# The first token tile's products of v for four pieces of weights, ahead of the second tile's x

## The chip, the cores and the metric

The kernel runs on one core of a Trainium2 chip. The metric is the device time of one execution in microseconds (us). TensorE (PE in the profile; PEld is its weight load) multiplies, VectorE (DVE), ScalarE (ACT) and GpSimd (POOL) work elementwise, SyncE (SP) issues the loads. Each engine works through its own instructions in the order of the program.

## The reference

One block of a network on `x` of 256 tokens by 1024 features, all in float32: an RMSNorm, a wide projection `w_in`, causal pooling and block attention side by side, gates, an output projection, and an MLP with squared ReLU.

```python
u = rmsnorm(h, norm_mix_pre[l])
z = u @ w_in[l]
p = z[..., :o_q]
q = z[..., o_q:o_k].reshape(B, S, N_HEADS, HEAD_DIM)
k = z[..., o_k:o_v].reshape(B, S, N_HEADS, HEAD_DIM)
v = z[..., o_v:o_g].reshape(B, S, N_HEADS, HEAD_DIM)
...
h = h + rmsnorm(m @ w_out[l], norm_mix_post[l])
u2 = rmsnorm(h, norm_mlp_pre[l])
a = jnp.square(jax.nn.relu(u2 @ w_up[l]))
h = h + rmsnorm(a @ w_down[l], norm_mlp_post[l])
```

What the change touches is the start: `v = u @ w_in[:, v columns]`, a product of 256 x 1024 by 1024 x 512.

## The kernel before, in words

**Three products for one.** Every float32 operand is split in a high part of reduced precision and a low part (operand minus high part). A product is then three matmuls: high by high, and the two mixed ones. `mm3` (L223) issues these three; in the text they are "a triple".

**The v stage.** The tokens lie in two tiles t = 0, 1 of 128 rows, the 1024 features in eight pieces k of 128. The weights of v are eight loads of 128 x 512 (`load_v(k)`, `v_r` in the trace, 256 KB each). x comes in four loads of 256 KB: `load_x(t, n)` takes tile t, half n of the features, so that half 0 serves k = 0 to 3 and half 1 serves k = 4 to 7. For v,

- `turn_x(t, n)` (L348) transposes four 128 x 128 blocks of x on TensorE into one PSUM bank (`x_ps`);
- `u_parts(k, t)` (L336) makes the two parts of u from that bank, scaled by the norm's gain: `uh` on ACT (L307), then `ul` on DVE (L308), which reads uh;
- `split_v(k)` (L351) splits a piece of weights: `v_h` on ACT (L89), then `v_l` (L93), of whose 512 columns DVE makes 352 and POOL 160;
- `v_rows(t, k)` (L341) is the triple that adds piece k into tile t's accumulator `v_ps`. It needs uh and v_h for its first matmul, both shares of v_l for the second and ul for the third (v_h, ul).

The 1/rms factor of a token is applied when v leaves PSUM, so the products don't wait for it. The whole program is written in the order that each engine follows (`manual_schedule`, L40): an instruction that waits holds up all that stand behind it on its engine. Some matmuls on constants (`keep_busy`, L59) fill TensorE until the first x has come.

**Loads.** SP issues all loads of weights and x on one queue. Eight semaphores are used in turn, so an issue waits until the load eight places ahead of it has landed. `load_next` (L145) issues the next block of weights of the list that begins with q, k and p; it takes one of three raw buffers and waits until the block in that buffer is split.

**Behind v.** The four pieces of q's weights are split (`q_h` on ACT, `q_l` on DVE and POOL) right behind the last `u_parts`; TensorE multiplies q (32 triples of 256 columns), then k, scores, p and so on. DVE makes the token norms between q_l and the splits of k's weights (`k_l`, L406), which are followed by what it takes out of q's and k's accumulators.

Of the kernel before, what the change touches and what calls it, by code (L numbers as in the profile page):

```python
# [20 lines left out]
KD = D // P  # L21
# [12 lines left out]
def hybrid_block(ctx: ExitStack, tc: tile.TileContext, x, norm_mix_pre, w_in, b_gate, pool_w, pool_scale,  # L34
# [110 lines left out]
    def load_next():  # L145
        if done[0] < len(order):
            order[done[0]].load_all()
            done[0] += 1
# [15 lines left out]
    def load_x(t, n):  # L164
        c = slice(n * 512, (n + 1) * 512)
        nc.sync.dma_start(x_sb[:, t, c], x[0, t * P:(t + 1) * P, c])


    class Columns:
# [12 lines left out]
        def turn(self):  # L182
            ps = bank(self.name + "_ps")
            nc.tensor.transpose(ps[:, 0:self.n], self.row, ident[0:self.n, 0:self.n])
            nc.vector.tensor_copy(self.col, ps[:, 0:self.n])
# [8 lines left out]
    def load_v(k):  # L194
        bv[k // 4].load(k % 4)

    load_x(0, 0)
    g_mix.load()
    load_v(0)
    load_v(1)  # L200
    load_x(1, 0)
    load_v(2)
    load_x(0, 1)
    load_v(3)
    load_x(1, 1)
    for k in range(4, KD):
        load_v(k)
    load_next()
    others.load()
# [13 lines left out]
    def mm3(ps, whl, rhl, start, stop, last=0):  # L223

        (wh, wl), (rh, rl) = whl, rhl
        second, third = ((wh, rl), (wl, rh)) if last == 0 else ((wl, rh), (wh, rl))
        nc.tensor.matmul(ps, wh, rh, start=start, stop=False, skip_group_check=True)  # L227
        nc.tensor.matmul(ps, *second, start=False, stop=False, skip_group_check=True)  # L228
        nc.tensor.matmul(ps, *third, start=False, stop=stop, skip_group_check=True)  # L229
# [12 lines left out]
    def tokens(hl, k, t):  # L242
        c = slice(t * P, (t + 1) * P)
        return hl[0][:, k, c], hl[1][:, k, c]
# [5 lines left out]
    def narrow(blocks, k, c=slice(0, 512)):  # L250
        b = blocks[k // 4]
        return b.hi[:, k % 4, c], b.lo[:, k % 4, c]
# [50 lines left out]
    def scaled_parts(hl, k, t, ps, gain):  # L303
        c = slice(t * P, (t + 1) * P)
        v = ps[:, (k % 4) * P:(k % 4 + 1) * P]
        hi, lo = hl[0][:, k, c], hl[1][:, k, c]
        nc.scalar.activation(hi, v, AF.Copy, scale=gain)  # L307
        nc.vector.scalar_tensor_tensor(lo, v, gain, hi.bitcast(F32), op0=ALU.mult, op1=ALU.subtract)  # L308
# [27 lines left out]
    def u_parts(k, t):  # L336
        scaled_parts(u, k, t, xT[t, k // 4], g_mix[k])
# [3 lines left out]
    def v_rows(t, k, last=0):  # L341
        mm3(vps[t], tokens(u, k, t), narrow(bv, k), k == 0, k == KD - 1, last)
# [5 lines left out]
    def turn_x(t, n):  # L348
        xT[t, n] = turn(x_sb[:, t, :], n, f"x_ps{t}{n}")

    def split_v(k):  # L351
        bv[k // 4].split_piece(k % 4, True)
# [5 lines left out]
    u_parts(0, 0)  # L358
    bv[0].share_lo(0)
    v_rows(0, 0, last=1)  # L360
    u_parts(1, 0)
    turn_x(1, 0)
    split_v(1)
    v_rows(0, 1)
    u_parts(0, 1)
    v_rows(1, 0)
    turn_x(0, 1)
    u_parts(1, 1)
    v_rows(1, 1)
    for k in range(2, KD):  # L370
        if k == 3:
            turn_x(1, 1)
        split_v(k)
        for t in range(NT):
            u_parts(k, t)
            v_rows(t, k)
        if k == 3:
            load_next()
    for b in bq:
        b.allot()  # L380
    bq[0].split_piece(0, True)
# [521 lines left out]
```

## Time and profile before

| | |
|---|---|
| median of 3 runs | 350.66 us (350.08 to 565.49) |
| the profiled execution, its own time | 350.98 us |
| its span, from first to last instruction | 349.2 us |
| mean granted TensorE clock | 0.992 |
| v's first matmul to its last (starts) | 5.57 to 19.68 us |
| q's first matmul | 20.18 us |

The profile counts time from the first instruction. In a line of the timeline the first number is an instruction's start, the second its duration; several alike in a row are put together (xN). What stands in brackets is the idle time of the engine just before, and what ended it. Matmuls are pipelined: a 128 x 512 one is shown with 0.39 us, and the next starts 0.23 us after it.

### The profile page before, as it was taken

The page shows a single profiled execution, that of the slowest core. Times are in us where ns is not written, and L with a number is a line of the kernel's source. Part 1 is how long each engine was busy: PE and PEld are TensorE (multiplying, and loading weights), DVE is VectorE, ACT ScalarE, POOL GpSimd, SP SyncE. Part 2 cuts the span into 40 slices and gives each one's busy share as a digit, 9 for nine tenths or more (in the row PEclk, how much of TensorE's full clock was granted, in tenths as well). Part 3 has the DMA queues.
Part 4 walks back from the last instruction along what each step waited for, and adds up shares of the span by engine and source line. Part 5 has one row for each costly group of instructions (what it writes and reads, how often), then busy time and mean ns, then how long its engine had stood idle before and what let it go on. Part 6 is the DMA issues. An engine that isn't in the chain of part 4 may idle for free.

```text
span 349.2 us, 5700 instructions
## 1 busy us (share of the span) xinstructions
PE 337.0 (96%) x2313; PEld 309.5 (89%) x2313; DVE 216.0 (62%) x284; ACT 182.0 (52%) x257; POOL 98.7 (28%) x80
## 2 busy tenths in 40 slices
PE   7999999999999999899999999999999999999991
PEld 6799999999999999678899898998989989899880
DVE  2889687995474476656677846537465374653545
ACT  3885657665557442447775635445254452544231
POOL 3599966143113088718530000000000000000000
PEclk9999999999999999999999999999999999999996
DMA  6996861552636636563467490935709358090003
GB/s 203 382 288 232 195 229 38 218 164 95 225 122 240 240 122 243 153 209 121 139 223 234 160 331 12 340 131 211 272 9 340 134 199 283 8 346 11 0 0 120
DMA packets 27506, 63.04 MB, mean 181 GB/s; under 512 B 1332, under 2 KB 3160, under 8 KB 27480
## 3 DMA queue, kind: packets, MB, share of 16 engines
q1 hardware_dynamic: 26904, 62.15, 51.3%
q0 software_dynamic: 576, 0.52, 1.1%
q8 instruction: 18, 0.29, 0.3%
q14 instruction: 8, 0.07, 0.1%
HBM read 61.10 MB, written 1.05 MB: 178 GB/s over the span
## 4 chain that ended last, share of the span: by engine, by line
PE 55%; DVE 1%; ACT 0%; DVEq 0%; issue 0%; ACTq 0%
PE up_ps L227 8%; PE up_ps L228 8%; PE up_ps L229 8%; PE d_ps L240 8%; PE d_ps L236 8%; PE d_ps L237 8%; PE wo_ps L240 1%; PE wo_ps L237 1%; PE wo_ps L236 1%; PE d_ps L229 1%; PE d_ps L228 1%; PE d_ps L227 1%; PE h_ps L300 0%; DVE o_out L848 0%; DVE ml L318 0%; PE wo_ps L228 0%
## 5 line engine op out<-in xcount | busy, mean ns | idle before, releaser
L227 PE MATMUL up_ps<-u2h,up_h 128*128 128x256 f32 x224 | 62.2, 278 | 0.0
L228 PE MATMUL up_ps<-u2l,up_h 128*128 128x256 f32 x224 | 62.0, 277 | 0.0
L229 PE MATMUL up_ps<-u2h,up_l 128*128 128x256 f32 x224 | 61.9, 277 | 0.0
L845 POOL TENSOR_TENSOR o_out<-o_out,g_mlp_post 128x256 f32<-128x256 f32 x2 | 1.5, 733 | 164.1 <-DVE rr L289 159.9
L236 PE MATMUL d_ps<-dn_h,ah 128*128 128x512 f32 x120 | 46.9, 391 | 0.0
L93 DVE TENSOR_TENSOR dn_l<-dn_r,dn_h 128x2048 fp32r<-128x2048 f32 x16 | 36.5, 2292 | 16.7 <-ACT dn_h L89 16.7
L237 PE MATMUL d_ps<-dn_l,ah 128*128 128x512 f32 x120 | 46.8, 390 | 0.0
L228 PEld LDWEIGHTS up_ps<-u2l,up_h 128*128 128x128 f32 x224 | 42.1, 188 | 0.3
L227 PEld LDWEIGHTS up_ps<-u2h,up_h 128*128 128x128 f32 x224 | 42.0, 188 | 0.3
L229 PEld LDWEIGHTS up_ps<-u2h,up_l 128*128 128x128 f32 x224 | 42.1, 188 | 0.0
L89 ACT ACTIVATE dn_h<-dn_r 128x2048 fp32r<-128x2048 f32 x16 | 30.5, 1916 | 21.5 <-issue 13.2
L240 PE MATMUL d_ps<-dn_h,al 128*128 128x512 f32 x120 | 37.4, 393 | 0.0
L227 PE MATMUL g_ps<-uh,g_h 128*128 128x256 f32 x128 | 36.6, 286 | 0.6 <-DVE pt L422 0.6
L229 PE MATMUL g_ps<-uh,g_l 128*128 128x256 f32 x128 | 36.2, 283 | 0.0
L228 PE MATMUL g_ps<-ul,g_h 128*128 128x256 f32 x128 | 36.2, 283 | 0.0
L93 DVE TENSOR_TENSOR up_l<-up_r,up_h 128x2048 fp32r<-128x2048 f32 (+1 forms) x14 | 30.2, 2194 | 8.1 <-ACT up_h L89 8.1
L89 ACT ACTIVATE up_h<-up_r 128x2048 fp32r<-128x2048 f32 x16 | 29.9, 1903 | 1.6 <-PE wo_ps L240 1.6
L758 ACT ACTIVATE relu<-up_ps 128x512 f32<-128x512 f32 x16 | 9.5, 594 | 39.8 <-PE up_ps L229 39.8
L760 DVE TENSOR_TENSOR a<-up_ps,relu 128x512 f32<-128x512 f32 x16 | 11.0, 690 | 29.2 <-ACT relu L758 29.1
L240 PEld LDWEIGHTS d_ps<-dn_h,al 128*128 128x128 f32 x120 | 22.5, 188 | 4.9
L237 PEld LDWEIGHTS d_ps<-dn_l,ah 128*128 128x128 f32 x120 | 22.5, 188 | 4.9
L236 PEld LDWEIGHTS d_ps<-dn_h,ah 128*128 128x128 f32 x120 | 22.5, 188 | 4.5
(226 smaller groups left out, 856.3 us busy)
## 6 DMA issues: line engine op xcount, KB each, us to landing
up_r<-in_w_up_dram SPq DMA_DIRECT2D x16, 1024.0 KB, 5.5
dn_r<-in_w_down_dram SPq DMA_DIRECT2D x16, 1024.0 KB, 5.1
g_r<-in_w_in_dram SPq DMA_DIRECT2D x8, 1024.0 KB, 5.8
o_r<-in_w_out_dram SPq DMA_DIRECT2D x4, 1024.0 KB, 4.9
v_r<-in_w_in_dram SPq DMA_DIRECT2D x8, 256.0 KB, 5.9
q_r<-in_w_in_dram SPq DMA_DIRECT2D x4, 512.0 KB, 6.4
k_r<-in_w_in_dram SPq DMA_DIRECT2D x2, 1024.0 KB, 6.1
p_r<-in_w_in_dram SPq DMA_DIRECT2D x2, 1024.0 KB
```

What stands on the lines that cost most here:

```text
L89: nc.scalar.activation(self.hi[:, s, :], self.raw[:, s, :], AF.Copy)
L93: eng.tensor_tensor(self.lo[:, s, c], self.raw[:, s, c], self.hi[:, s, c].bitcast(F32), ALU.subtract)
L227: nc.tensor.matmul(ps, wh, rh, start=start, stop=False, skip_group_check=True)
L228: nc.tensor.matmul(ps, *second, start=False, stop=False, skip_group_check=True)
L229: nc.tensor.matmul(ps, *third, start=False, stop=stop, skip_group_check=True)
L236: nc.tensor.matmul(ps, xh, wh[:, c], start=start, stop=False, skip_group_check=True)
L237: nc.tensor.matmul(ps, xh, wl[:, c], start=False, stop=False, skip_group_check=True)
L240: nc.tensor.matmul(ps, xl, wh[:, c], start=False, stop=stop, skip_group_check=True)
L758: nc.scalar.activation(r, ps, AF.Relu)
L760: nc.vector.tensor_tensor(a, ps, r, ALU.mult)
L845: nc.gpsimd.tensor_tensor(o[:, 768:D], o[:, 768:D], g_mlp_post[:, 768:D], ALU.mult)
```

## The change

The loads of v's pieces 2 and 3 are issued ahead of the second tile's x (and of the first tile's second half). The products of tile 0 with pieces 1 to 3 then run ahead of everything of tile 1. Tile 1 follows with its pieces 0 to 3 in a row; its transpose now stands directly ahead of its first product, and the transpose of its second half directly ahead of its product with piece 4. From piece 5 on the order is that of before. No instruction is added or removed; behind v the order is the same.

```diff
     load_x(0, 0)
     g_mix.load()
-    load_v(0)
-    load_v(1)
+    for k in range(4):
+        load_v(k)
     load_x(1, 0)
-    load_v(2)
     load_x(0, 1)
-    load_v(3)
+    load_v(4)
     load_x(1, 1)
-    for k in range(4, KD):
+    for k in range(5, KD):
         load_v(k)
     load_next()
...
     v_rows(0, 0, last=1)
-    u_parts(1, 0)
+
+    for k in range(1, 4):
+        u_parts(k, 0)
+        split_v(k)
+        v_rows(0, k)
+    load_next()
     turn_x(1, 0)
-    split_v(1)
-    v_rows(0, 1)
     u_parts(0, 1)
     v_rows(1, 0)
-    turn_x(0, 1)
     u_parts(1, 1)
     v_rows(1, 1)
-    for k in range(2, KD):
-        if k == 3:
-            turn_x(1, 1)
-        split_v(k)
+    turn_x(0, 1)
+    u_parts(2, 1)
+    v_rows(1, 2)
+    split_v(4)
+    u_parts(3, 1)
+    v_rows(1, 3)
+    u_parts(4, 0)
+    v_rows(0, 4)
+    turn_x(1, 1)
+    split_v(5)
+    u_parts(4, 1)
+    v_rows(1, 4)
+    for k in range(5, KD):
+        if k > 5:
+            split_v(k)
         for t in range(NT):
             u_parts(k, t)
             v_rows(t, k)
-        if k == 3:
-            load_next()
```

On SP, at the start of the program, before and then after. `x_sb` is x, `v_r` a piece of v's weights:

```order
L166 DMA x_sb<-in_x_dram 128x512
L179 DMA g_mix_row<-in_norm_mix_pre_dram 8x128
L80 DMA v_r<-in_w_in_dram 128x512 x2
L166 DMA x_sb<-in_x_dram 128x512
L80 DMA v_r<-in_w_in_dram 128x512
L166 DMA x_sb<-in_x_dram 128x512
L80 DMA v_r<-in_w_in_dram 128x512
L166 DMA x_sb<-in_x_dram 128x512
L80 DMA v_r<-in_w_in_dram 128x512 x4
```

```order
L166 DMA x_sb<-in_x_dram 128x512
L179 DMA g_mix_row<-in_norm_mix_pre_dram 8x128
L80 DMA v_r<-in_w_in_dram 128x512 x4
L166 DMA x_sb<-in_x_dram 128x512 x2
L80 DMA v_r<-in_w_in_dram 128x512
L166 DMA x_sb<-in_x_dram 128x512
L80 DMA v_r<-in_w_in_dram 128x512 x3
```

Of the twelve loads of 256 KB, tile 1's first half of x moves from the fourth place to the sixth, pieces 2 and 3 from the fifth and seventh to the fourth and fifth.

On TensorE, behind the first triple of v, before: the transposes of x (`x_ps10` is tile 1, half 0; `x_ps01` tile 0, half 1) and the triples of tile 0 (`v_ps0`) and tile 1 (`v_ps1`):

```order
L300 MATMUL x_ps10_192<-ident_110,x_sb_115 128x128 x4
L227 MATMUL v_ps0_159<-v_0_h_161,uh_155 128x512
L228 MATMUL v_ps0_159<-v_0_l_162,uh_155 128x512
L229 MATMUL v_ps0_159<-v_0_h_161,ul_156 128x512
L227 MATMUL v_ps1_160<-v_0_h_161,uh_155 128x512
L228 MATMUL v_ps1_160<-v_0_l_162,uh_155 128x512
L229 MATMUL v_ps1_160<-v_0_h_161,ul_156 128x512
L300 MATMUL x_ps01_208<-ident_110,x_sb_115 128x128 x4
```

And in the changed kernel, the last of three triples of tile 0 in a row and what follows it:

```order
L226 MATMUL v_ps0_159<-v_0_h_161,uh_155 128x512
L227 MATMUL v_ps0_159<-v_0_l_162,uh_155 128x512
L228 MATMUL v_ps0_159<-v_0_h_161,ul_156 128x512
L299 MATMUL x_ps10_217<-ident_110,x_sb_115 128x128 x4
L226 MATMUL v_ps1_160<-v_0_h_161,uh_155 128x512
L227 MATMUL v_ps1_160<-v_0_l_162,uh_155 128x512
L228 MATMUL v_ps1_160<-v_0_h_161,ul_156 128x512
```

Three triples now stand ahead of tile 1's transpose, and no triple of tile 0 between that transpose and the first triple that reads its result. The same holds further on for the second half (`x_ps11`):

```order
L228 MATMUL v_ps0_159<-v_4_h_163,ul_156 128x512
L299 MATMUL x_ps11_255<-ident_110,x_sb_115 128x128 x4
L226 MATMUL v_ps1_160<-v_4_h_163,uh_155 128x512
L227 MATMUL v_ps1_160<-v_4_l_164,uh_155 128x512
L228 MATMUL v_ps1_160<-v_4_h_163,ul_156 128x512
```

Before, a triple of tile 0 stood between these transposes and the triple of tile 1 that needs them.

## Rows read from the trace of the kernel before

**Rows 1.** The page, part 1: busy us, share of the span, instructions of each engine.

```profile
PE 337.0 (96%) x2313; PEld 309.5 (89%) x2313; DVE 216.0 (62%) x284; ACT 182.0 (52%) x257; POOL 98.7 (28%) x80
```

**Rows 2.** Waits of TensorE, whole span: us in total, times, longest us.

```profile
PE wo_ps L236 <- ACT mh L317: 1.0, 1, 1.0
...
PE wo_ps L237 <- POOL o_l L93: 0.7, 1, 0.7
PE g_ps L227 <- DVE pt L422: 0.6, 1, 0.6
```

**Rows 3.** Timeline of TensorE in the v stage and behind it.

```profile
6.56 0.47 PE L229 MATMUL v_ps<-v_l,uh 128*128 128x512 f32 x1 [0.26 <-DVE v_l L93]
7.93 0.66 PE L300 MATMUL x_ps<-ident,x_sb 128*128 128x128 f32 x4 [0.90 <-DMA x_sb<-in_x_dram]
8.35 0.48 PE L227 MATMUL v_ps<-v_h,uh 128*128 128x512 f32 x1
...
12.65 0.60 PE L300 MATMUL x_ps<-ident,x_sb 128*128 128x128 f32 x4
13.00 0.47 PE L227 MATMUL v_ps<-v_h,uh 128*128 128x512 f32 x1
...
20.00 0.24 PE L184 MATMUL others_ps<-ident,others_row 28*128 28x28 f32 x1
20.18 0.39 PE L227 MATMUL q_ps<-uh,q_h 128*128 128x256 f32 x1
...
31.91 0.36 PE L227 MATMUL k_ps<-uh,k_h 128*128 128x256 f32 x1
```

**Rows 4.** Timeline of ScalarE in the v stage.

```profile
5.98 0.62 ACT L89 ACTIVATE v_h<-v_r 128x512 fp32r<-128x512 f32 x1
8.63 0.37 ACT L307 ACTIVATE uh<-x_ps,g_mix_col 128x128 fp32r<-128x128 f32 x1 [2.03 <-PE x_ps L300]
9.41 0.37 ACT L307 ACTIVATE uh<-x_ps,g_mix_col 128x128 fp32r<-128x128 f32 x1 [0.42 <-DVE ul L308]
...
12.09 0.63 ACT L89 ACTIVATE v_h<-v_r 128x512 fp32r<-128x512 f32 x1 [0.21 <-DMA v_r<-in_w_in_dram]
...
13.29 0.37 ACT L307 ACTIVATE uh<-x_ps,g_mix_col 128x128 fp32r<-128x128 f32 x1 [0.30 <-PE x_ps L300]
...
16.61 3.99 ACT L89 ACTIVATE q_h<-q_r 128x1024 fp32r<-128x1024 f32 x4
```

**Rows 5.** Timeline of GpSimd, then of VectorE, same stretch and behind it.

```profile
6.67 0.86 POOL L93 TENSOR_TENSOR v_l<-v_r,v_h 128x160 fp32r<-128x160 f32 x1 [0.65 <-ACT v_h L89]
...
17.79 6.04 POOL L93 TENSOR_TENSOR q_l<-q_r,q_h 128x320 fp32r<-128x320 f32 x4 [0.59 <-ACT q_h L89]
...
5.60 0.82 DVE L93 TENSOR_TENSOR v_l<-v_r,v_h 128x352 fp32r<-128x352 f32 x1
...
26.03 0.16 DVE L286 RECIPROCAL r<-sq 128x1 f32<-128x1 f32 x1 [0.88 <-ACT sq L281]
...
28.10 5.09 DVE L93 TENSOR_TENSOR k_l<-k_r,k_h 128x2048 fp32r<-128x2048 f32 x2
...
60.16 1.27 DVE L422 TENSOR_TENSOR pt<-p_ps,rrow 128x512 f32<-128x512 f32 x2
```

**Rows 6.** Issues on SP's queue, fifth and sixth load; then each one's us to landing.

```profile
2.94 0.43 SPq L80 DMA_DIRECT2D v_r<-in_w_in_dram  x1
3.41 0.43 SPq L166 DMA_DIRECT2D x_sb<-in_x_dram  x1
...
v_r<-in_w_in_dram SPq DMA_DIRECT2D x1, 256.0 KB, 5.6
x_sb<-in_x_dram SPq DMA_DIRECT2D x1, 256.0 KB, 6.6
```

**Rows 7.** Windows: stretch, its length, busy us (instructions) by engine, granted clock, DMA share, GB/s.

```profile
7.00:8.00 1.00, 0.10 (x2) 0.07 (x2) 0.16 (x1) 0.00 (x0) 0.53 (x1) 1.00 0.86 279
...
343.00:344.00 1.00, 0.00 (x0) 0.00 (x0) 0.90 (x5) 0.56 (x2) 0.08 (x1) 0.77 0.00 0
```

## The prediction

> **What bounds the kernel now.** I read four things in this order. The page's first part [rows 1]: TensorE is busy for 337.0 of 349.2 us, so nothing but TensorE's own idle time and the length of its work can move the end. TensorE's waits [rows 2]: behind the start only small ones are left, 1.0, 0.7 and 0.6 us being the longest. So a change in the v stage is worth what it does to the moment at which TensorE gets through that stage, unless one of these later waits takes it back. The timeline of TensorE [rows 3] then shows the stage itself: the first triple ends at 6.56 + 0.23 = 6.79, the transpose of tile 1's x waits for its load until 7.93, and from there TensorE is dense: ten triples between 13.00 and 20.00, 0.70 us each (0.69 without the slower restart behind a transpose), and a transpose costs 0.35 to 0.45 (12.65 to 13.00; 7.93 to 8.35). The hole of 1.14 us from 6.79 to 7.93 is all that the new order can fill. Last, the timelines of ACT, POOL and DVE [rows 4, 5] show what a triple needs before it can run.
>
> **Loads.** The change moves loads between places of one queue, all of 256 KB, so I let a place keep its landing time. The fourth load, now x of tile 1, lands at 7.9 [rows 3]; the fifth at 2.94 + 5.6 = 8.5 and the sixth at 3.41 + 6.6 = 10.0 [rows 6]; the ninth, weight piece 4, ends a wait of ACT at 12.1 [rows 4]; the two between them at 10.7 and 11.4 by equal steps. After the change piece 2 lands at 7.9, piece 3 at 8.5, tile 1's x at 10.0, tile 0's second half at 10.7, piece 4 at 11.4, tile 1's second half at 12.1. SP's later issues keep their places; those that wait for a raw buffer wait for the splits.
>
> **The triples of tile 0, one by one.** Piece 1 has been split as before: POOL is done with its share at 6.67 + 0.86 = 7.53 [rows 5]. A matmul starts about 0.15 us after the part it waits for (DVE's share of piece 0 ends at 5.60 + 0.82 = 6.42 [rows 5], the matmul starts at 6.56 [rows 3]). The triple (tile 0, piece 1) can start at 6.79, waits 0.6 before its second matmul until 7.68, and ends at 8.14. For piece 2 the chain starts only at its landing: 7.9, plus 0.62 on ACT [rows 4], is 8.55, plus 0.87 on POOL is 9.45. Its triple starts at 8.7, waits again before the second matmul until 9.6, and ends at 10.06. Piece 3 is then held by POOL, which takes 0.87 a piece: 10.32; the triple ends at 10.93. So three triples (2.07 us of work) fill the stretch 6.79 to 10.93, 4.1 us: the hole of before has become three waits of 0.6, 1.2 and 0.2 us.
>
> **The transposes.** Tile 1's transpose starts at 10.93, its x having landed. In the trace ACT starts on a fresh bank 0.70 us after the first transpose (7.93 to 8.63), and uh takes 0.37 [rows 3, 4]. Before, a triple of tile 0 ran in that gap. Now the next triple is the one that reads this uh: it starts at 10.93 + 0.70 + 0.37 + 0.15, about 12.2, where the transposes alone would have let it start at 11.4. That is 0.8 us of new idle time. Along one bank, uh of the next piece waits for ul of the one before (0.42 in [rows 4], a period of 0.78), which stays hidden behind a triple's 0.69 as long as uh is one piece ahead; without that cover it costs 0.1 a piece, for at most two pieces, and I take nothing. From 12.2: two triples, a transpose, three triples, which bring TensorE to 16.2. The second exposed transpose follows, with uh on ACT at 16.88 and the triple at 17.5 (again 0.8 idle). Seven triples of 0.69 are left: 22.3, where [rows 3] has 20.0. **TensorE is 2.3 us late at the end of the v stage.** The count of instructions is the same, so the whole of it is waiting: 2.0 + 0.8 + 0.8 less the 1.14 (and some restart time) of before.
>
> **The other engines.** ACT is held by the same transpose: the first uh of the second half goes from 13.29 to 16.88 [rows 4]; from there to q_h were 3.3 us, of which one weight split (0.52) now lies earlier, and the bank's waits give some 0.2 back. q_h starts near 19.9 instead of 16.61, 3.3 us late, and with it POOL's and DVE's q_l (POOL from 17.79 to about 21.1 [rows 5]). POOL ended q_l at 23.83; the first matmul that needs its last piece is the 42nd of q, at 20.18 + 41 x 0.122 = 25.2 (96 matmuls between 20.18 and 31.91). The cover of 1.2 us takes the 1.0 by which POOL is later than TensorE. Nothing is added there, with 0.2 left. DVE's norms and k_l come next. k_l ends at 28.10 + 5.09 = 33.19, and the fifth triple of k reads its second half at 31.91 + 14 x 0.12 + 0.1 = 33.7: 0.35 of cover. DVE comes 3.3 us late, or less if its wait of 0.88 for ACT [rows 5] shrinks, so 2.4 to 3.3. Against TensorE's 2.3 + 0.35 that adds 0 to 0.65; I take 0.3, the middle, since ACT is late as well. From k on DVE and TensorE run in step, and the wait of 0.6 at the gates is one for DVE [rows 2], whose evacuation at 60.16 [rows 5] comes as late as its chain.
>
> **Sum.** 2.3 + 0.3 = 2.6 us on the profiled execution's 350.98, which is 353.6. That execution stands 0.3 above the median of the runs, so 353.4 is my figure for the measurement, 0.8% slower.
>
> **The clock.** Between 6.79 and 12.2 TensorE now works for 2.5 us of 5.4. In the trace a hole of 1.14 us left the granted clock at 1.00, and it fell, to 0.77 over a microsecond, only in the tail, where TensorE had been idle since 341.5 [rows 7]. No new hole is longer than 0.9, so the sum has nothing for the clock. The Trainium skill, "TensorE: Matmul & The Clock Gate", section "HAM oscillation — how this bites in real kernels", speaks against that: bursts of matmuls with waits between them can let the clock fall back from 2.4 to 1.2 GHz, each burst then starting slow. By that rule this change would pay once more, as the second rival has it; by the rows it does not.
>
> **Rivals.**
> *Given back further on.* TensorE's delay meets later waits that were not its own: 0.6 at the gates, 1.0 and 0.7 at the output projection [rows 2]. If DVE and ACT caught up by then, 2.3 of delay would be absorbed and the time would be 350.7, not slower than before. The point that decides is DVE's evacuation at 60.16: it must not move. For it: DVE is busy only 62% of the span. Against it: its chain hangs on the same late ACT, and the waits at the output projection are for products of TensorE itself. With the 0.6 alone the time is 353.0, still within my forecast. 13%.
> *The clock falls.* The waits of 6.8 to 12.2 cost the granted clock. At the lower level a triple takes 0.69 us more; three triples make 2.1, all twelve that are left 8.3. 355.7 to 362, likeliest 356. Against it stands [rows 7]. 8%.
> *The hole is filled.* If pieces 2 and 3 landed right behind piece 1, at steps of 0.7 (6.3 and 7.0), the products would wait less. But POOL's 0.87 a piece and the two exposed transposes stay: the three triples would end near 10.0 and the v stage at 21.3, 1.3 late. That is a time of 352.1, the low end of my own case. Only if the matmul did not wait for POOL's share and ACT's uh came faster would 1.14 be won: 349.6. 5%.
> The order of the rows shows that the change does what it says, so that rival falls away.
>
> **Chances and range.** My forecast, 74%: landings one step of 0.7 earlier or later and the 0 to 0.65 of DVE make it 351.9 to 354.9. Reaching to most of the first rival and to the low end of the second, 8 times in 10 it is 351.2 to 355.4. 2% is 7 us, about what a measurement of this kernel can tell from no change. Nothing above wins 7 us: faster 1%. Only a clock that stays low for the whole stage loses as much: slower 4%. Within 2%: 95%.
>
> **What would show it.** Right: TensorE's waits list v_ps behind POOL's or ACT's part for some 2 us in all and two waits of v_ps for uh of about 0.8; the transpose of tile 1 starts near 10.9, q's first matmul near 22.5, q_h on ACT near 20. k's fifth triple waits for DVE a little, and the gates' wait for DVE is still there. The granted clock reads 1.00 from 7 to 13. Wrong: piece 2's wait ends well before 7.9, so that a place does not keep its landing time; TensorE's delay at q is under 1 us; or the delay is there at q and gone at 61.

## The result, and the profile after

The changed kernel takes 353.62 us (median of 4 runs, 353.25 to 353.77) against 350.45 us for the kernel before on the same chip, 3.2 us more. The ratio is 1.0085 [1.0068, 1.0103], 3.0 us; one of the four executions of before took 565.49 us, which stands in the median and not in the ratio. The forecast was 353.4. The profiled execution took 353.53 us, its span is 351.8 us and its mean granted clock 0.996; the span of before's was 349.2. So the two traces differ by 2.6 us and the medians by 3.2; the first experiment shows where the rest can come from.

The page of the changed kernel, part 1, beside [rows 1]: busy time and instruction counts are as they were (TensorE 1.0 us more busy, 2313 instructions in both). The loss is waiting.

```profile
PE 338.0 (96%) x2313; PEld 309.0 (88%) x2313; DVE 216.5 (62%) x284; ACT 182.4 (52%) x257; POOL 98.8 (28%) x80
```

The waits of TensorE in the changed kernel (us in total, times, longest), to be laid beside [rows 2]:

```profile
PE g_ps L226 <- DVE pt L432: 0.9, 1, 0.9
PE v_ps L226 <- ACT uh L306: 0.9, 2, 0.5
...
PE k_ps L228 <- DVE k_l L93: 0.4, 1, 0.4
PE v_ps L227 <- POOL v_l L93: 0.3, 1, 0.3
```

The wait for tile 1's x is gone. New are the waits of v for uh (two of them) and for POOL's part, as forecast, and one in k; the wait at the gates has grown from 0.6 to 0.9. The two at the output projection (`wo_ps`, 0.9 and 0.7) are within 0.1 of what they were.

TensorE's timeline in the changed kernel, to be laid beside [rows 3], and behind it the gates' first matmul in the trace of before:

```profile
6.99 0.40 PE L226 MATMUL v_ps<-v_h,uh 128*128 128x512 f32 x1
7.72 0.50 PE L227 MATMUL v_ps<-v_l,uh 128*128 128x512 f32 x1 [0.33 <-POOL v_l L93]
...
9.66 0.50 PE L227 MATMUL v_ps<-v_l,uh 128*128 128x512 f32 x1
...
10.23 0.60 PE L299 MATMUL x_ps<-ident,x_sb 128*128 128x128 f32 x4
11.28 0.50 PE L226 MATMUL v_ps<-v_h,uh 128*128 128x512 f32 x1 [0.46 <-ACT uh L306]
...
15.39 0.60 PE L299 MATMUL x_ps<-ident,x_sb 128*128 128x128 f32 x4
16.45 0.50 PE L226 MATMUL v_ps<-v_h,uh 128*128 128x512 f32 x1 [0.46 <-ACT uh L306]
...
21.64 0.38 PE L226 MATMUL q_ps<-uh,q_h 128*128 128x256 f32 x1
...
33.39 0.36 PE L226 MATMUL k_ps<-uh,k_h 128*128 128x256 f32 x1
...
35.75 0.39 PE L228 MATMUL k_ps<-uh,k_l 128*128 128x256 f32 x1 [0.44 <-DVE k_l L93]
...
63.38 0.39 PE L226 MATMUL g_ps<-uh,g_h 128*128 128x256 f32 x1 [0.92 <-DVE pt L432]
```

```profile
60.89 0.39 PE L227 MATMUL g_ps<-uh,g_h 128*128 128x256 f32 x1 [0.61 <-DVE pt L422]
```

Three triples of tile 0 fill 6.99 to 10.23; from each transpose to the triple behind it TensorE needs 1.05 us; q begins 1.46 us later than before, k 1.48 later, and the gates 2.49 later. Behind the gates nothing more happens: from their first matmul to the start of TensorE's last one it is 280.3 us in this trace and 280.2 in that of before. So the 2.5 us come in two places, 1.46 in the v stage and 1.0 between k and the gates.

The same trace, ScalarE, to be laid beside [rows 4]:

```profile
7.10 0.62 ACT L89 ACTIVATE v_h<-v_r 128x512 fp32r<-128x512 f32 x1
...
8.03 0.63 ACT L89 ACTIVATE v_h<-v_r 128x512 fp32r<-128x512 f32 x1
...
10.86 0.37 ACT L306 ACTIVATE uh<-x_ps,g_mix_col 128x128 fp32r<-128x128 f32 x1 [2.20 <-PE x_ps L299]
...
19.12 3.92 ACT L89 ACTIVATE q_h<-q_r 128x1024 fp32r<-128x1024 f32 x4
...
26.34 1.92 ACT L89 ACTIVATE k_h<-k_r 128x2048 fp32r<-128x2048 f32 x1 [0.85 <-POOL q_l L93]
```

The splits of weight pieces 2 and 3 (7.10 and 8.03) do not wait for their loads at all; q_h is 2.5 us later than before. The last row's wait is put down to POOL's q_l; a run below shows that it was the load of k. The chain to it can be read on the other engines, to be laid beside [rows 5]; behind them SP's issue of k's first load in the trace of before:

```profile
18.81 0.88 POOL L93 TENSOR_TENSOR v_l<-v_r,v_h 128x160 fp32r<-128x160 f32 x1 [0.16 <-ACT v_h L89]
...
19.72 4.03 SPq L80 DMA_DIRECT2D k_r<-in_w_in_dram  x2
...
28.46 0.17 DVE L285 RECIPROCAL r<-sq 128x1 f32<-128x1 f32 x1 [0.82 <-ACT sq L280]
...
30.60 5.09 DVE L93 TENSOR_TENSOR k_l<-k_r,k_h 128x2048 fp32r<-128x2048 f32 x2
```

```profile
17.22 4.03 SPq L80 DMA_DIRECT2D k_r<-in_w_in_dram  x2
```

k's weights take the raw buffer of v's second half. Their first load is issued at 19.72, right when POOL ends its share of v's last piece (18.81 + 0.88); before that was at 17.22. It lands 6.5 us later, and k_h starts (26.34). ACT's square roots for the norms stand behind k_h, DVE's reciprocals wait for those, and k_l stands behind them: 30.60 where [rows 5] has 28.10, 2.5 us late.

The granted clock of the changed kernel in the stretch behind the first bare transpose, beside [rows 7]:

```profile
11.00:12.00 1.00, 0.72 (x3) 0.48 (x3) 0.35 (x1) 0.58 (x2) 0.00 (x0) 1.00 1.07 404
```

It reads 1.00, the 2.4 GHz level, there and in every other stretch from 4 to 20 us, through all the new waits.

### The profile page after: what moved, and what is told of

Its sections match the earlier page's. It is cut to its first block, busy times and chain, and to the rows that moved or that the text cites. A ratio compares the mean times of both kernels' runs of the same rounds, so it can differ in the third digit from the quotient of the medians.

```text
span 351.8 us, 5699 instructions
## 1 busy us (share of the span) xinstructions
PE 338.0 (96%) x2313; PEld 309.0 (88%) x2313; DVE 216.5 (62%) x284; ACT 182.4 (52%) x257; POOL 98.8 (28%) x80
## 3 DMA queue, kind: packets, MB, share of 16 engines
HBM read 61.10 MB, written 1.05 MB: 177 GB/s over the span
## 4 chain that ended last, share of the span: by engine, by line
PE 54%; DVE 1%; ACT 0%; DVEq 0%; issue 0%; ACTq 0%
PE up_ps L226 8%; PE up_ps L227 8%; PE up_ps L228 8%; PE d_ps L239 8%; PE d_ps L235 8%; PE d_ps L236 8%; PE wo_ps L239 1%; PE wo_ps L236 1%; PE wo_ps L235 1%; PE d_ps L228 1%; PE d_ps L227 1%; PE d_ps L226 1%; PE h_ps L299 0%; DVE o_out L858 0%; DVE ml L317 0%; PE wo_ps L227 0%
```

## The experiments

A transpose is called covered when a triple that does not need its result stands behind it, and bare when the next triple waits for it. Theory 1, held at the start: whatever delays tile 1's transposes (bare, or behind a late x) delays uh and so ScalarE, and ScalarE's first split of q is what reaches the end. Its rivals: only TensorE's own lateness counts; theory 2, the new load order does it, whatever the work; theory 3, the order of the triples does it, whatever the loads. Theory 1 did not last: its figures came out for several runs, and the two kernels that make TensorE and ScalarE late one at a time then refuted the way it took to the end. Twelve runs, each beside the kernel before on its chip.

### The kernel before, once more

No edit.

> The kernel before, profiled once more. It tells which landing times in the first 15 us belong to the places in the queue and which to one execution. In the first profile one of the 16 shares of a load came 0.85 us behind the other 15 (fifteenth share at 9.19, last at 10.04 for the sixth load); in the changed kernel's profile the last share is 0.25 behind. If that straggling share belongs to the execution, this profile shows another lag for the same order, q's first split on ScalarE (16.61 in the first profile) moves by as much as the landings do, to 15.9 with no lag, and the span follows by up to 0.8 us. If it belongs to the order of the loads, everything reads as in the first profile within 0.1 us.

Measured: 350.31 us, span 348.5. TensorE's timeline in this execution:

```profile
7.30 0.66 PE L300 MATMUL x_ps<-ident,x_sb 128*128 128x128 f32 x4 [0.20 <-DMA x_sb<-in_x_dram]
...
19.48 0.39 PE L227 MATMUL q_ps<-uh,q_h 128*128 128x256 f32 x1
...
60.18 0.39 PE L227 MATMUL g_ps<-uh,g_h 128*128 128x256 f32 x1 [0.59 <-DVE pt L422]
```

The first alternative holds: the straggling share belongs to the execution. The wait of 0.90 in front of tile 1's transpose [rows 3], which makes the hole of 1.14 us, is 0.20 here, q begins 0.70 earlier, ScalarE's first split of q at 15.91, and the span is 0.7 shorter. Against this execution the changed kernel is 2.16 late at q and 3.20 at the gates; against the first it was 1.46 and 2.49. The loss by the ratio (3.0) and by the medians (3.2) lies between 2.49 and 3.20, nearer to the second. Three later traces with the loads and the order of before at this place show the wait again: 1.42 (TensorE late), 0.30 (ScalarE late) and none with four raw buffers, which waits 0.93 in front of the next transpose instead. So the hole comes and goes from one execution to the next, between nothing and more than the one that the change was built to fill.

### The order of loads alone, and the order of work alone

The first kernel has the new loads and the work in before's order, the second the new order of work on the old loads:

```
 loads_only:  load x00, v0, v1, v2, v3, x10, x01, v4, x11, v5...   work as before
 order_only:  load x00, v0, v1, x10, v2, x01, v3, x11, v4...       work as after
```

> The new order of the loads under the old order of the work. Theory 1 (ScalarE's first split of q is what reaches the end: whatever delays the transposes of the second tile delays uh, then ScalarE, VectorE and GpSimd, and TensorE ends up as late as they): tile 1's x lands at 9.2, TensorE's hole behind the first triple grows from 1.1 to about 2.5, q's first split starts near 18.0 and q's first matmul near 21.4; 352.2 us, 1.8 above before. Theory 2 (the whole loss comes from the loads, the order of the triples being free): 353.6 as the changed kernel. Theory 3 (the loss is all in the order of the triples with the two bare transposes): 350.4.

Measured: 354.68 us, 1.0111 [1.0076, 1.0145]. All the figures expected were too low. TensorE's timeline and a window of this kernel:

```profile
9.69 0.86 PE L299 MATMUL x_ps<-ident,x_sb 128*128 128x128 f32 x4 [2.68 <-DMA x_sb<-in_x_dram]
```

```profile
12.00:13.00 1.00, 1.00 (x4) 0.65 (x3) 0.83 (x4) 1.00 (x4) 0.66 (x1) 0.50 1.04 391
```

Two places further back, tile 1's x makes TensorE wait 2.68 us, and just behind that wait the clock falls: it is granted at 0.50 (1.2 GHz) from 10.0 to about 13.4. The rival of the prediction that the clock falls is real, in this neighbour of the change. The three triples of tile 0 are thus worth something: the change, which puts them into that hole, takes 353.62 and keeps the clock, with its two bare transposes; with these covered (turns_early below, 351.18) the same loads cost 3.5 us less than here.

> The new order of the work with the old order of the loads: tile 0's triples with pieces 2 and 3 wait for loads that stand behind tile 1's x. By the landing times of before (piece 2 at 7.9 to 8.5, piece 3 at 9.5 to 10.7) TensorE ends v near 23.4 to 24.2 and the gates follow 40.7 us behind; 355.5 to 356.5, some 2 above the changed kernel. If the order of the work costs what it costs by the two bare transposes alone, whatever the loads: 353.6. If the granted clock falls, as it did for 3.4 us with the new loads under the old order, another 1 to 1.7.

Measured: 356.28 us, 1.0170 [1.0109, 1.0230]. That is the median of 354.57, 354.76, 357.81 and 358.36, two pairs 3 us apart; it lies in the range given for a clock that holds, but the clock falls, and the profiled execution, the 354.57, is below both ranges. What sets the other pair 3 us higher no trace here shows. In the one traced q begins at 24.60. The triple of tile 0 with piece 2 waits for its weights, that with piece 3 no longer does, and the clock is down from 10.2 to about 13.7:

```profile
9.43 0.49 PE L227 MATMUL v_ps<-v_h,uh 128*128 128x512 f32 x1 [0.78 <-ACT v_h L89]
```

```profile
11.00:12.00 1.00, 1.00 (x4) 0.55 (x3) 0.31 (x1) 0.00 (x0) 0.70 (x1) 0.50 1.04 391
```

Neither half of the change is any good alone. The Trainium skill, "TensorE: Matmul & The Clock Gate", section "HAM oscillation — how this bites in real kernels", which the prediction weighed, tells of a kernel whose bursts of matmuls lose the clock in the waits for a load between them. Those waits are longer than any in these v stages, so its rule does not reach this change, and the prediction read it too widely when it had the change pay by it. The trace of loads_only agrees in kind (0.50 behind a wait of 2.68 us for a load). That of order_only loses the clock with no wait above 1.13 us, which that section does not cover, and that of the change, whose longest wait there is 0.5, keeps it.

### Covering the transposes again

The change's loads and its three early triples stay; only the transposes move, so that each is covered again.

```diff
 turn0_early
     for k in range(1, 4):
         u_parts(k, 0)
         split_v(k)
+        if k == 3:
+            turn_x(1, 0)
         v_rows(0, k)
     load_next()
-    turn_x(1, 0)
```

```diff
 turn1_early
     u_parts(3, 1)
+    turn_x(1, 1)
     v_rows(1, 3)
     u_parts(4, 0)
     v_rows(0, 4)
-    turn_x(1, 1)
```

turns_early has both.

> The changed kernel with the transpose of tile 1's second half two triples earlier, ahead of the product of tile 1 with piece 3; its x has landed by then (11.2 against about 14). Theory 1: ScalarE's uh of that bank starts near 14.7 instead of 16.02, TensorE's wait of 0.7 for it is gone, q's first split starts at 17.8 instead of 19.12 and the time falls by about 1.4 to 352.2 although TensorE itself gains only 0.8 at q. If only TensorE's own waits count: 0.8 less, 352.8. Theory 2 (the loads alone): unchanged, 353.6.

> The changed kernel with tile 1's first transpose alone moved up, ahead of tile 0's product with piece 3. Theory 1: its wait of 0.7 for uh is covered, TensorE and ScalarE both come 0.9 earlier (q's first split at 18.2 instead of 19.12); 352.7. Theory 2 (the loads alone): 353.6.

> As the last, and in addition tile 1's first transpose ahead of tile 0's product with piece 3, so that a triple of tile 0 again covers the way from each transpose to the triple that reads it. Theory 1: both bare transposes are covered, q's first split starts near 17.0, q's first matmul near 20.1; 351.1 to 351.4 us, 0.7 to 1 above before, what is left being the later x. If only TensorE's own waits count: 1.6 less than the changed kernel, 352.0. Theory 2: 353.6.

Measured: turn1_early 352.14 us, 1.0041 [1.0025, 1.0057]; turn0_early 352.52, 1.0055 [1.0040, 1.0071]; turns_early 351.18, 1.0016 [1.0001, 1.0030]; all three near what theory 1 expected, and two of them below the figure that stood for TensorE's own waits alone. By the ratios the second transpose gives back 1.5 of the 3.0 us, the first 1.1, both 2.4. TensorE's timeline with both early:

```profile
9.43 0.60 PE L299 MATMUL x_ps<-ident,x_sb 128*128 128x128 f32 x4
9.79 0.49 PE L226 MATMUL v_ps<-v_h,uh 128*128 128x512 f32 x1
...
20.06 0.39 PE L226 MATMUL q_ps<-uh,q_h 128*128 128x256 f32 x1
```

From a transpose to the next triple it is 0.36 us again, where the change needs 1.05; q_h (16.94) and k_l (27.25) are back to about where the two traces of before have them (15.91 and 16.61; 27.36 and 28.10), and q begins 0.58 later than in the second. The 0.6 us that are left by the ratio fit that, and TensorE's waits here are those of the three triples for their splits; no run isolates it.

### Two pieces instead of four

The loads of x for tile 1 one place later only, with tile 0's triple of piece 1 ahead of the transpose and that of piece 2 behind it (several lines written as one):

```diff
-    load_v(0); load_v(1); load_x(1, 0); load_v(2); load_x(0, 1)
+    load_v(0); load_v(1); load_v(2); load_x(1, 0); load_x(0, 1)
...
     v_rows(0, 1)
+    u_parts(2, 0); split_v(2); turn_x(1, 0); v_rows(0, 2)
```

> A milder form of the change: only piece 2 is loaded ahead of tile 1's x, tile 0's products with pieces 1 and 2 fill the hole, and the transposes stay covered (tile 1's stands ahead of tile 0's product with piece 2). Theory 1: TensorE's hole is filled, but ScalarE, which has to make the same 16 uh and 7 v_h, reaches q's first split within 0.2 of before (16 to 16.7), so the time stays at 350.4, within 0.4. If filling TensorE's hole is what pays: 349.6. If loading weights ahead of tile 1's x costs by itself: above 351.

Measured: 350.49 us, 0.9995 [0.9986, 1.0004]. As theory 1 expected: the smallest form of the idea costs nothing and wins nothing. In its trace the transpose starts at 8.04 without a wait, so the hole is filled; why that pays nothing, though some executions of before have the hole, is not shown.

### TensorE late by itself, ScalarE late by itself

The kernel before, once with 18 idle matmuls on TensorE between v and q, once with two idle copies on ScalarE ahead of q's split:

```diff
 pe_late                          act_late, act_late2
+    keep_busy(18)                +    for _ in range(2):
     others.turn()                +        idle = junk.tile([P, 512], BF16, name="scr_a")
                                  +        nc.scalar.activation(idle, x_sb[:, 0, 0:512], AF.Copy)
                                       bq[0].split_piece(0, True)
```

> The kernel before with 18 matmuls of 128 columns on constants between v and q: about 1.0 us of work for TensorE alone, no other engine is touched. Theory 1 (behind v the end follows ScalarE's and VectorE's chain, not TensorE): TensorE is 1.0 late at q, its wait for VectorE at the gates (0.6) vanishes, and 0.4 is left at the end; 350.8. Rival (TensorE's own delay goes through to the end): 351.4.

Measured: 351.90 us, 1.0035 [1.0021, 1.0048], 1.4 us more. Theory 1's smaller figure is refuted and the rival's is the nearer. TensorE's timeline in this kernel:

```profile
8.22 0.66 PE L300 MATMUL x_ps<-ident,x_sb 128*128 128x128 f32 x4 [1.42 <-DMA x_sb<-in_x_dram]
...
20.14 1.23 PE L61 MATMUL busy<-const-bfloat16-1.0 128*128 128x128 bf16 x18
21.48 0.39 PE L227 MATMUL q_ps<-uh,q_h 128*128 128x256 f32 x1
...
62.19 0.39 PE L227 MATMUL g_ps<-uh,g_h 128*128 128x256 f32 x1 [0.59 <-DVE pt L423]
```

q begins 1.30 later than in the trace of before (about 1.1 for the idle matmuls, 0.2 for the longer wait for x), and so do the gates, whose wait for DVE is still 0.59. DVE's evacuation came 1.30 later as well (61.46 against 60.16). That wait is no slack: what DVE evacuates there hangs on TensorE's own products. So nothing is given back at the gates, and the prediction's first rival falls for a lateness of TensorE.

> The kernel before with two dummy copies of 128 x 512 on ScalarE ahead of q's first split: about 1.05 us of work for ScalarE alone; TensorE's instructions are as before. Theory 1: q is not held (1.2 us of cover), but k's fifth triple waits for VectorE by 0.6 to 0.7 and the gates by the rest; 351.4, the whole delay. Rival (what hides ScalarE at q hides it for good): 350.4.

Measured: 349.66 us, 0.9976 [0.9965, 0.9987]: not slower but faster, against both theories. A second set of runs of the same kernel gives the trace for it.

> The same kernel as the earlier one with ScalarE delayed ahead of q's first split, for a profile of it. Revised theory (two chains meet at the gates: TensorE from q's first matmul, +40.7 us, and k's weights from their landing; k's first load may only start when the raw buffer of v's second half has been split): the dummy work delays q's split by 1.05, but not the split of v's last piece, so k's load starts and lands as before (issue near 17, landing 23 to 24) and k's first split on ScalarE starts at 23.5 to 24.0, not 1.05 later; the time is that of before within 0.4. First theory (ScalarE's first split of q reaches the end): 1.0 later; it is already against the measured time.

Measured: 349.79 us, 0.9984 [0.9967, 1.0000], span 347.7; k's load and split come as the revised theory expected. ScalarE, SP and TensorE in this kernel, then ScalarE and SP in the second execution of before:

```profile
17.12 3.88 ACT L89 ACTIVATE q_h<-q_r 128x1024 fp32r<-128x1024 f32 x4
...
23.50 1.92 ACT L89 ACTIVATE k_h<-k_r 128x2048 fp32r<-128x2048 f32 x1
...
16.50 5.20 SPq L80 DMA_DIRECT2D k_r<-in_w_in_dram  x2
...
59.44 0.28 PE L227 MATMUL g_ps<-uh,g_h 128*128 128x256 f32 x1
```

```profile
15.91 3.93 ACT L89 ACTIVATE q_h<-q_r 128x1024 fp32r<-128x1024 f32 x4
...
22.95 1.92 ACT L89 ACTIVATE k_h<-k_r 128x2048 fp32r<-128x2048 f32 x1 [0.66 <-DMA k_r<-in_w_in_dram]
...
16.52 4.03 SPq L80 DMA_DIRECT2D k_r<-in_w_in_dram  x2
```

q_h is 1.2 later than in the second execution of before, but k's load is issued where it was, and k_h starts only 0.55 later; k_l, at 27.40 against 27.36, is not late at all. So 1.2 us of lateness of ScalarE at q do not reach the end, and theory 1 falls. That points to the other thing that is late in the change, v's last split, which frees the buffer for k's load. The change makes q_h later than that, by 3.2 against this execution of before; the next run shows what such a lateness does without the buffer.

### A fourth raw buffer

What v's split holds up is a buffer. With four raw buffers instead of three, k's load no longer waits for v's second half; an unused tile made the room (its line is not shown).

```diff
-    wraw = ctx.enter_context(tc.tile_pool(name="wraw", bufs=3))
+    wraw = ctx.enter_context(tc.tile_pool(name="wraw", bufs=4))
```

> The changed kernel with four raw buffers for weights in place of three (an unused tile of 8 KB is dropped for the room). k's first load then waits for the split of v's first half, not of its second. Revised theory: k's weights have landed long before ScalarE comes to them; k's first split starts at 25.4 instead of 26.34, TensorE's wait for k_l (0.44) and the excess of 0.3 at the gates go, and the gates start 1.0 earlier, held by TensorE alone; 352.6. If k's load is not what holds the second chain: unchanged, 353.6.

> The kernel before with four raw buffers, the control of the last. Revised theory: in the kernel before both chains arrive together (60.65 by either), so freeing one leaves TensorE's: 350.5, no change within 0.3. If four buffers help by themselves (deeper loads further on): both kernels with four fall by the same amount.

Measured: on the change 351.76 us, 1.0031 [1.0010, 1.0052], 1.9 less than the change where 1.0 was expected; on the kernel before 350.41, 1.0003 [0.9993, 1.0013], nothing, as expected. SP, ScalarE, GpSimd and TensorE of the change with four buffers:

```profile
12.86 6.78 SPq L80 DMA_DIRECT2D k_r<-in_w_in_dram  x2
...
24.95 1.90 ACT L89 ACTIVATE k_h<-k_r 128x2048 fp32r<-128x2048 f32 x1
...
19.84 6.05 POOL L93 TENSOR_TENSOR q_l<-q_r,q_h 128x320 fp32r<-128x320 f32 x4 [0.58 <-ACT q_h L89]
...
21.15 0.39 PE L226 MATMUL q_ps<-uh,q_h 128*128 128x256 f32 x1
...
61.10 0.28 PE L226 MATMUL g_ps<-uh,g_h 128*128 128x256 f32 x1
```

The load goes out at 12.86 instead of 19.72, and k_h starts at 24.95, while POOL is at q_l until 25.89: the wait of 0.85 that the change's profile put down to q_l was for the load. The gates start 2.28 earlier than in the change. By the rule of the table below, 0.49 of that is q's earlier start in this execution (tile 1's transpose starts 0.46 earlier already), 1.04 is the difference by which k's chain had come after TensorE's, and 0.75 comes from DVE further on (last section). The run shows that the buffer is worth 1.9 us to the change and nothing to the kernel before; that k's chain is about 1.0 of it is read from the traces. With the buffer free, the late q_h (18.67) still carries on to k_l (28.99), which is then just level with TensorE: 28.99 + 32.8 = 61.79 against 21.15 + 40.7 = 61.85. So ScalarE's late queue alone brings k no later than TensorE is, and the load is what goes beyond.

How the two chains meet, over the traces: the gates' first matmul comes 40.7 us after q's first or 32.8 us after DVE starts k_l, whichever is later.

| trace | q first | + 40.7 | k_l | + 32.8 | gates, measured |
|---|---|---|---|---|---|
| before | 20.18 | 60.88 | 28.10 | 60.90 | 60.89 |
| before, second execution | 19.48 | 60.18 | 27.36 | 60.16 | 60.18 |
| TensorE late | 21.48 | 62.18 | 27.14 | 59.94 | 62.19 |
| after | 21.64 | 62.34 | 30.60 | 63.40 | 63.38 |
| first transpose early | 20.57 | 61.27 | 30.00 | 62.80 | 62.80 |
| second transpose early | 20.64 | 61.34 | 27.84 | 60.64 | 61.36 |

The two constants are read off the first row; the other five rows test them, the second constant only where k comes later (after, first transpose early). Of the other seven traces, four (loads_only, turns_early, two_pieces, before with four buffers) follow the rule within 0.1, and in three the gates start 0.75 earlier (last section). The early transposes bring both chains forward: k's load is issued at 18.69, 18.11 and 17.53 with the first, the second and both early, against 19.72. So theory 1 had those times right by a path that was not the one.

## Why the prediction was right

The time and the direction came as forecast; of the parts, two were off, and the sum was right partly by luck.

**What bounds it.** Right: busy times stayed, the v stage's lateness went to the end, and nothing behind the gates gave any back.

**Loads.** "A place keeps its landing time" failed as a step. Pieces 2 and 3 were to land at 7.9 and 8.5; their splits start at 7.10 and 8.03 without a wait. The prediction had named a piece 2 well before 7.9 as a sign of being wrong. A place does not keep its landing time even under one order: tile 1's x, in the fourth place, let its transpose start at 7.93, 7.30 and 8.22 in three executions.

**The triples of tile 0.** The order of events was right, the size not: the three triples were to run from 6.79 to 10.93, with 2.0 us of waits; they ran from 6.99 to 10.23, 3.24 us for 2.07 of work, so 1.2 us of waits. With the pieces there early, POOL's 0.87 to 0.93 a piece sets their pace, which the prediction had for piece 3 alone. This is the term that was mis-sized most.

**The transposes.** Right: two waits for uh, 1.05 us from transpose to triple where a covered one has 0.35 to 0.42. That is 0.7 each, with 0.8 forecast. The covered versions show that they matter more than that: 2.4 us go with them, because the late second half also holds up ScalarE's splits of v's last pieces, and with them k's load.

**The v stage as a whole.** 2.3 forecast; 1.46 against the execution that the sum was made on, 2.16 against the second. The first had given the kernel before a hole of 1.14, and with it q 0.7 later than the second; the prediction subtracted that hole as a gain of the new order.

**q and k.** q was not held up: from q's first matmul to k's first it is 11.75 us after and 11.73 before. k was to add 0 to 0.65, taken as 0.3; it added 1.0, beyond the bound. The step that failed is the sentence that SP's issues which wait for a raw buffer "wait for the splits": it named the wait and gave it no price. The prediction sent k's lateness through q_h, POOL's and DVE's queues. ScalarE made late by 1.2 shows nothing of it at the end, and with the fourth buffer that path brings k no later than TensorE; the load that waits for the buffer is what adds the 1.0.

**The sum.** 2.6 forecast for the span and 2.6 measured, by two errors that cancel: 0.8 too much in the v stage, 0.7 too little at k. That is luck. Against the second execution of before it is 2.16 + 1.04 = 3.2. The direction and the v stage were understood; the figure was better than its parts.

**The rivals.** Given back: refuted by the late TensorE, which paid for its whole lateness. The clock falls: not in this kernel (1.00), but in both halves of it, so 8% was not too much. The hole is filled: in the v stage this rival, given 5%, came nearest, with the triples ending near 10.0 and 1.3 late against 10.23 and 1.46 measured; its 352.1 lacked what k adds. Its hope of a gain is answered by two_pieces, which fills the hole without the bare transposes and is level with before.

**Which version is best.** The kernel before with two idle copies on ScalarE, 0.9976 and 0.9984 of its time in two sets of runs, is the fastest that was run, by 0.6 to 0.8 us, though the second interval reaches 1.0000. The best form of the change that was run, both transposes early, is still 1.0016 [1.0001, 1.0030].

## What to carry to other kernels

A transpose, a copy and a product that needs it formed a chain of 1.05 us here: keep independent work between them, and when you move work forward, look at what it had been covering. A late stage reaches the end by more than one way: besides the queues, follow the buffer that its last step sets free and the load that waits for it. And a hole seen in one execution should be looked for in several (0.90, 0.20, 1.42, 0.30 here) before a change is built to fill it.

## What was not expected of the hardware

DVE's second p_l, an instruction of one shape, has two durations. The second execution of before, DVE's two and GpSimd's two, and then the same of the kernel with ScalarE late; GpSimd's lines give shortest, median and longest in ns, then the two starts:

```profile
41.24 1.62 DVE L93 TENSOR_TENSOR p_l<-p_r,p_h 128x1408 fp32r<-128x1408 f32 x1 [1.00 <-ACT p_h L89]
43.04 2.74 DVE L93 TENSOR_TENSOR p_l<-p_r,p_h 128x1408 fp32r<-128x1408 f32 x1 [0.18 <-ACT p_h L89]
...
L93 POOL TENSOR_TENSOR p_l<-p_r,p_h x2: 2828/2884/2940, 41.5 to 44.3; 128x640 fp32r<-128x640 f32 x2
```

```profile
43.05 1.67 DVE L93 TENSOR_TENSOR p_l<-p_r,p_h 128x1408 fp32r<-128x1408 f32 x1 [0.17 <-ACT p_h L89]
...
L93 POOL TENSOR_TENSOR p_l<-p_r,p_h x2: 1574/1928/2281, 43.9 to 46.1; 128x640 fp32r<-128x640 f32 x2
```

Running side by side is not enough to slow DVE down: in the first execution its first p_l overlaps POOL's and still takes 1.62. It had begun before POOL's; the second p_l begins while POOL's first is under way (41.47 to 44.30) and takes 2.74. The rows fit an order in which the one that began later gets going only when the other ends: 44.30 + 1.62 is 45.9 for the end of DVE's second, which is 45.78, and POOL's two take 2.83 and 2.94 there, where the one that overlaps no p_l of DVE's takes 1.57. Where POOL begins only as DVE is half done, DVE keeps its 1.67, and POOL's first takes 2.28. In the three traces with the short form (ScalarE late, four buffers on the change, new order on old loads) the gates start 0.75 earlier than the table's rule gives and their wait for DVE is gone; that fits the gain of the idle copies and a part of that of the fourth buffer. The Trainium skill, "GPSIMD Engine Reference", section "8. Key points", says that GpSimd shares its SBUF interfaces with VectorE and contends with instructions of two SBUF inputs, which p_l is; these rows agree, with 1.07 us for this shape. That the overlap is the cause is read from the traces and was not isolated by a run of its own.

The other surprise is how little lies between keeping the clock and losing it: a single wait of 1.42 us (TensorE late) and the change's own pattern left it at 1.00; a single wait of 2.68 us, and the new order of work on the old loads with no wait above 1.13 us, brought it to 0.50. What decides between them stays open.
